# A decoder trunk step: another order of the first loads, the first squares later, and the second run of state steps one tile sooner

## The chip, the cores and the metric

The kernel runs on one core of a Trainium2 chip. The metric is the device time of one execution in microseconds. Two kernels are compared by the medians of their runs. One execution of each is taken with the hardware profiler; its trace gives the rows that are quoted. In them PE is TensorE's matmuls, PEld its weight loads, DVE VectorE, ACT ScalarE, POOL GpSimd, SP SyncE; a "q" behind an engine's name (SPq) is its sequencer issuing a DMA.

## The reference

One inference step of a trunk with a single layer: 512 new positions of one prompt and one new position of each of 8 samples, 520 columns in all, of 1024 channels, in fp32.

```python
h = h + 0.5 * swiglu(rms_norm(h, ffn1_norm), ffn1_w_gate, ffn1_w_up, ffn1_w_down)
h = h + hybrid_mixer(rms_norm(h, mix_norm), ...)      # pooling mixer and Mamba-2 SSD mixer side by side
h = h + 0.5 * swiglu(rms_norm(h, ffn2_norm), ffn2_w_gate, ffn2_w_up, ffn2_w_down)
y = rms_norm(h, final_norm)
# swiglu(x, wg, wu, wd) = (silu(x @ wg) * (x @ wu)) @ wd, with 2816 hidden channels
# outputs: y of prompt and samples, and the new pooling, convolution and SSM states of both
```

The new SSM state of a sample is state * decay + (dt * x) outer B, for 16 heads of 64 x 128.

## The kernel before, in words

**Layout.** `h` keeps the residual stream in SBUF, channels on the 128 partitions: 8 tiles of [128, 520], named by `d`. A tile of columns is halved (2 x 260). Tile d of the input x comes by one DMA from SP's queue (L500; the first one brings the vectors of parameters as well).

**An FFN.** There are 22 gate/up tiles `f` of 128 hidden channels each. The raw weights of one, `raw_f`, are two halves of [128, 1024] fp32, the gate's (u = 0) and the up's (u = 1); `raw` has two buffers, so a load waits until the tile two places before it has been used up. For most tiles the product is made in fp32r: every operand is split into a high part (a cast on ScalarE, L113) and a low part (a subtraction on VectorE, L114), `mm3` makes three matmuls of them (L124, L127, L128: high x high, high x low, low x high), and a scheme of seven products instead of eight combines column halves and weight halves (products 1 to 7 into the banks A and BE). For that the weights are summed first on VectorE (`sums`, L305 to L307, tiles `s`), and the sums are split too: `whi_fa`, `whi_fb` are casts of raw weights, `shi_fc`/`slo_fc` and `shi_fd`/`slo_fd` those of the sums. Copies of banks on ScalarE (`ac`, L344) let a bank be used again.

**The prologue.** Since normalised, split input isn't ready at once, FFN1's first two tiles, f = 0 and f = 1, are made in plain fp32 (`plain`, L254) from `xg`, which is x times the norm's weights without the root of the mean square; that factor is put on afterwards. One plain call is a matmul of 260 columns that shows as two records. The loop over j = 0..3 (L497 to L507) treats the pair of x tiles (j, j+4). For each j it does, as written: load both x tiles; load that part of raw_0 which this pair needs, u0 and u1, 128 KB each (L240; for j = 0 both from ScalarE's queue, else from SP's); scale (`scaled`, L192, ScalarE); square and sum the squares (`squares`, L161 and L164 on ScalarE, L165 on VectorE); the plain calls of f = 0, four of u0 and four of u1; and `prep_pair`, which forms the differences of the seven products and splits them into `xth`, `xtl` (L198 to L207, VectorE and ScalarE; the last pair's second half is kept for later, `late`). Then raw_1 is loaded (L236), the sum of squares goes through a matmul with ones (L170, tile `psr`) for each column half, ScalarE takes the root (L171), VectorE the reciprocal, and ScalarE copies the banks P of f = 0 into `tg` and `ac` (`keep`, L264; L267 for f = 1). The plain calls of f = 1 take the banks tagged A for u = 0 and the tag BE, which has two buffers, for u = 1: so these calls need the banks of f = 0 copied. The tile f = 2 follows by the seven products.

**The order.** The program is written in one order, and a scheduler decides each engine's own order from its idea of durations; `high_priority` moves a piece ahead, `queued(ins)` puts a piece behind the given instructions in an engine's order, `keep_in_program_order` pins one. On the chip every engine then runs its list strictly in order, and waits for what it needs.

**Down and the states.** `down` adds up the hidden tiles in chunks of 8, 8 and 6 (c = 0, 1, 2); in each it goes over the 8 output tiles d: load the weights, split them (`whi_d`, `wlo_d`), matmuls into the bank `dn`, then `td` and the addition to h on VectorE (L414, L418). In FFN2 the steps of `new_states` (L890 to L914) are put between these tiles, 16 in all, 8 in each of the first two chunks. `STATES[d]` says how many steps stand ahead of tile d. A step loads the broadcast row `br` and the state `hs` of the step after next from GpSimd's queue (L893, L895), makes four `so` on ScalarE (L909) and four `hs` on VectorE (L911), and writes `hs` out from GpSimd's queue (L913).

Of the kernel before, what the change touches and what calls it, by code (L numbers as in the profile page):

```python
# [11 lines left out]
AF = mybir.ActivationFunctionType  # L12
# [8 lines left out]
NT = SEQ + NS  # L21
HB = NT // 2
HALVES = (slice(0, HB), slice(HB, NT))
KD = D // P
# [9 lines left out]
CHUNKS = (8, 8, 6)  # L34
NG = 9
ON_ACT = 4
STATES = (0, 1, 1, 1, 2, 1, 1, 1)

CONV_PLAN = (
    "b0 b1 d0 b2 b3 x0 x1 v0 d1 x2 x3 d2 X0 p0 y0 c0 A0 p1 x4 m0 x5 B0 c1 p2 m1 A1 x6 c2 p3 A2 B1 x7 "  # L40
# [18 lines left out]
NVEC = _o  # L59
# [3 lines left out]
def tile_trunk_step(ctx: ExitStack, tc: tile.TileContext, ins: dict, outs: dict):  # L63
    nc = tc.nc

    def pool(name, side, **kw):
        return tc.alloc_tile_pool(name=name, bufs=1, side=side, reuse_waits="tile", **kw)
# [11 lines left out]
    vx = act.tile([P, NVEC + KD * NT], F32, tag="h", name="h")  # L79
# [3 lines left out]
    def v(name, i, n=P):  # L83
        return vec[:n, VEC[name] + i : VEC[name] + i + 1]
# [6 lines left out]
    def queued(*ins):  # L91
        stack = ExitStack()
        for i in ins:
            stack.enter_context(tc.issue_after(i))
        return stack
# [4 lines left out]
    half, ends = [], []  # L100
# [17 lines left out]
    def load_unit(src, n, name):  # L118
        raw = raw_tile(name)[:, :n]
        nc.sync.dma_start(out=raw, in_=src)  # L120
        return split(raw, n, name, wp, 3, ("whi", "wlo"))

    def mm3(ps, whi, wlo, xhi, xlo, start, stop, pin=False, **kw):
        first = nc.tensor.matmul(ps, whi, xhi, start=start, stop=False, **kw)  # L124
        if pin:
            tc.keep_in_program_order(first)
        nc.tensor.matmul(ps, whi, xlo, start=False, stop=False, **kw)  # L127
        nc.tensor.matmul(ps, wlo, xhi, start=False, stop=stop, **kw)  # L128

    def ws(w, k, m=P):  # L130
        return w[:, k * m : (k + 1) * m]
# [27 lines left out]
    def squares(nx, wx, d, name):  # L159
        if d == 0:  # L160
            nc.scalar.activation(out=nx[2], in_=h[:, d], func=AF.Square)  # L161
            return
        sq = wx.tile([P, 2, HB], F32, tag="tg", bufs=2, name=f"sq_{name}_{d}").rearrange("p b t -> p (b t)")
        nc.scalar.activation(out=sq, in_=h[:, d], func=AF.Square)  # L164
        nc.vector.tensor_tensor(out=nx[2], in0=nx[2], in1=sq, op=ALU.add)  # L165
# [17 lines left out]
    def new_xt(xp, name):  # L183
        return (xp.tile([P, KD // 2, 7, HB], F32R, tag="xth", name=f"xth_{name}"),
                xp.tile([P, KD // 2, 7, HB], F32R, tag="xtl", name=f"xtl_{name}"), *stat(name))

    def scaled(gp, nb, norm, j, name, halves=False):
        xg = gp.tile([P, 4, HB], F32, tag="g", bufs=nb, name=f"xg_{name}{j}")
        for d, out in ((j, xg[:, 0::3]), (j + KD // 2, xg[:, 1:3])):
            hd = h[:, d].rearrange("p (b t) -> p b t", b=2)  # L190
            for s in (slice(0, 1), slice(1, 2)) if halves else (slice(0, 2),):
                nc.scalar.activation(out=out[:, s], in_=hd[:, s], func=AF.Copy, scale=v(norm, d))  # L192
        return xg

    def prep_pair(nx, gp, nb, xg, j, name, late=None):
        xth, xtl, _, _ = nx
        xd = gp.tile([P, 4, HB], F32, tag="g", bufs=nb, name=f"xd_{name}{j}")
        nc.vector.tensor_tensor(out=xd[:, 0:2], in0=xg[:, 0::2], in1=xg[:, 3:4].to_broadcast([P, 2, HB]),  # L198
                                op=ALU.subtract)
        nc.vector.scalar_tensor_tensor(out=xd[:, 2], in0=xd[:, 1], scalar=-1.0, in1=xg[:, 0], op0=ALU.mult,  # L200
                                       op1=ALU.subtract)
        last = nc.vector.scalar_tensor_tensor(out=xd[:, 3], in0=xd[:, 2], scalar=-1.0, in1=xg[:, 1], op0=ALU.mult,
                                              op1=ALU.subtract)

        def parts(s, t):
            cast = nc.scalar.copy(xth[:, j, t], s)
            low = nc.vector.tensor_tensor(out=xtl[:, j, t], in0=s, in1=xth[:, j, t].bitcast(F32), op=ALU.subtract)  # L207
            return cast.ins, low.ins

        parts(xg[:, 0:3], slice(0, 3))  # L210
        if late is not None:
            late.append(lambda: parts(xd, slice(3, 7)))
            return None
        return last.ins, *parts(xd, slice(3, 7))

    class Ffn:
# [180 lines left out]
        def down(self, c, lo, hi, after):  # L397
            n = hi - lo
            banks, units = {}, {}

            def part(d, ks):
                if d not in units:
                    units[d] = load_unit(ins[f"w{self.i}d"][d, :, lo * P : hi * P], n * P, f"{self.i}d{d}_{c}")
                    banks[d] = ps[0].tile([P, 2, 512], F32, tag="BE", bufs=2, name=f"dn{self.i}_{d}_{c}")
                wh, wl = units[d]
                for b in range(2):
                    for k in ks:
                        g = self.g[lo + k]
                        mm3(banks[d][:, b, :HB], ws(wh, k), ws(wl, k), g[:, 0, b], g[:, 1, b], k == 0, k == n - 1)

            def done(d):
                t = self.wx.tile([P, 2, HB], F32, tag="tg", bufs=2, name=f"td{self.i}_{d}_{c}")
                hd = h[:, d].rearrange("p (b t) -> p b t", b=2)
                nc.vector.scalar_tensor_tensor(out=t, in0=banks[d][:, :, :HB], scalar=-0.5,  # L414
                                               in1=self.nx[3].rearrange("p (b t) -> p b t", b=2), op0=ALU.mult,
                                               op1=ALU.mult)
                if after is None:
                    nc.vector.tensor_tensor(out=hd, in0=t, in1=hd, op=ALU.add)  # L418
                    return
                for b, hs in enumerate(HALVES):  # L420
                    nc.vector.tensor_tensor(out=h[:, d, hs], in0=t[:, b], in1=h[:, d, hs], op=ALU.add)
                    after(d, b, hs)

            first = 0
            if after is not None:
                part(0, range(n - 1))
                part(1, range(n - 1))
                part(0, range(n - 1, n))
                done(0)
                part(1, range(n - 1, n))  # L430
                done(1)
                first = 2
            for d in range(first, KD):
                for _ in range(STATES[d] if self.states is not None else 0):
                    next(self.states)
                part(d, range(n))
                done(d)
# [51 lines left out]
    wx1, g1 = pool("wx1", "right"), pool("g1", "right")  # L489
    ffn_psum("ppf1")  # L490
    nx1 = new_xt(xt1, "f1")
    ffn1 = Ffn(nx1, 1, wx1, g1, 2)
    xg1, late = [], []
    warm = bank("warm")
    for _ in range(8):
        nc.tensor.matmul(warm[:, :P], ones, ones, start=True, stop=True)
    for j in range(KD // 2):  # L497
        for d in (j, j + KD // 2):
            q = slice(NVEC + d * NT if d else 0, NVEC + (d + 1) * NT)
            nc.sync.dma_start(out=vx[:, q], in_=ins["x"][:, q])  # L500
        ffn1.plain_load(0, j, queue=nc.sync if j else nc.scalar)
        xg1.append(scaled(g1, NG, "ffn1_norm", j, "f1", not j))
        with tc.high_priority() if j else nullcontext():
            for d in (j, j + KD // 2):
                squares(nx1, wx1, d, "f1")
        ffn1.plain(0, xg1[j], j)
        prep_pair(nx1, g1, NG, xg1[j], j, "f1", late if j == KD // 2 - 1 else None)  # L507
    ffn1.plain_load(1)
    with tc.high_priority():
        root, recip = ffn1.scales()  # L510
# [38 lines left out]
    def fin(d, b, hs):  # L549
        nx = f2["ffn"].nx  # L550
        if b:
            with tc.high_priority():
                squares(nx, f2["wx"], d, "f2")
        j = d - KD // 2
        if j >= 0 and b:
            f2[j] = scaled(f2["xg"], 4, "ffn2_norm", j, "f2")
# [37 lines left out]
    todo, late = [], []  # L594
# [589 lines left out]
```

## Time and profile before

| | |
|---|---|
| median of 3 runs | 989.91 us (987.9 to 990.07) |
| the profiled execution | 989.39 us |
| its span in the trace | 987.5 us |
| PE busy | 971.4 us, 98% of the span |
| DVE, ACT, POOL busy | 81%, 56%, 9% |
| HBM traffic | 116 GB/s over the span |

The span runs from the first recorded instruction to the last; 1.89 us lie around it. The rows of a timeline are: start, duration, engine, line, operation, output <- inputs, shapes, the number of instructions put together in the row, and in brackets the idle time of the engine before it and what ended that. A row of the waits view has the waiting engine, tile and line, what it waited for, the sum in us, the number of times, and the longest. A row of the chain has start, duration and what the chain ran through. A row of the DMA view has the transfer, the queue, how many, the size of each, and the median time from issue to landing. A row of the windows view has the window, its length, the busy time of PE, PEld, DVE, ACT and POOL with the number of instructions, TensorE's granted clock, the busy share of the DMA engines, and GB/s.

### The profile page before, as it was taken

The numbers are of one execution on the slowest core, as the hardware profiler recorded it, in microseconds if no ns is written. First come the engines' busy times: TensorE is split into PE (matmuls) and PEld (weight loads), VectorE is DVE, ScalarE is ACT, GpSimd is POOL, SyncE is SP. The second block draws the span as 40 slices with busy tenths as digits, with TensorE's granted clock in tenths as the row PEclk, the third lists the DMA queues.
The fourth block names the chain that finished last, engine by engine and source line by source line (L and its number), as shares of the span: only waits on it lengthen the run. The fifth ranks groups of instructions, "written<-read, shape, count | busy, mean of one in ns | idle before, by whom it ended". The sixth has DMA issues, their size and how long they took to land.

```text
span 987.5 us, 19451 instructions
## 1 busy us (share of the span) xinstructions
PE 971.4 (98%) x7868; PEld 952.7 (96%) x7868; DVE 797.8 (81%) x1288; ACT 555.7 (56%) x1019; POOL 89.6 (9%) x160
## 2 busy tenths in 40 slices
PE   8999999999999999999999999999999999999996
PEld 7999999999999999999899999999999999999995
DVE  6999656997569688789978997999967899668876
ACT  7766414664136455685668574666643566534653
POOL 0000000000000000156512000200012000120000
PEclk9999999999999999999999999999999999999998
DMA  5423322323222232262335232523346423453222
GB/s 181 167 90 103 112 87 85 129 86 129 86 87 81 91 126 88 82 199 106 124 113 188 73 134 86 151 103 129 110 122 197 150 94 121 123 180 121 93 65 88
DMA packets 42459, 115.53 MB, mean 117 GB/s; under 512 B 6456, under 2 KB 13560, under 8 KB 42368
## 3 DMA queue, kind: packets, MB, share of 16 engines
q1 hardware_dynamic: 38320, 103.52, 30.6%
q0 software_dynamic: 3504, 10.49, 4.0%
q8 instruction: 62, 1.02, 0.4%
q10 hardware_dynamic: 544, 0.26, 0.1%
q14 instruction: 29, 0.24, 0.1%
HBM read 106.91 MB, written 7.34 MB: 116 GB/s over the span
## 4 chain that ended last, share of the span: by engine, by line
PE 91%; DVE 4%; DMA 2%; ACT 1%; issue 1%; POOL 1%; DVEq 0%; ACTq 0%; SPq 0%
PE A L128 8%; PE A L124 8%; PE A L127 8%; PE dn L128 7%; PE dn L124 7%; PE dn L127 7%; PE BE L128 6%; PE BE L127 6%; PE BE L124 6%; PE P L254 4%; PE wo L124 2%; PE wo L128 2%; PE wo L127 2%; PE inz L124 2%; PE inz L128 2%; PE inz L127 2%
## 5 line engine op out<-in xcount | busy, mean ns | idle before, releaser
L127 PE MATMUL dn<-g,whi_1d 128*128 128x260 f32 x352 | 99.4, 282 | 0.0
L124 PE MATMUL dn<-g,whi_1d 128*128 128x260 f32 x352 | 99.2, 282 | 0.2 <-DVE td L414 0.2
L128 PE MATMUL dn<-g,wlo_1d 128*128 128x260 f32 x352 | 99.3, 282 | 0.0
L414 DVE SCALAR_TENSOR_TENSOR td<-dn,r_f 128x520 f32<-128x520 f32 x40 | 27.9, 699 | 72.7 <-PE dn L128 72.7
L128 PE MATMUL dn<-g,wlo_2d 128*128 128x260 f32 x256 | 72.6, 283 | 0.9 <-DVE wlo_2d L114 0.9
L127 PE MATMUL dn<-g,whi_2d 128*128 128x260 f32 x256 | 72.3, 282 | 0.0
L124 PE MATMUL dn<-g,whi_2d 128*128 128x260 f32 x256 | 72.3, 282 | 0.0
L124 PEld LDWEIGHTS dn<-g,whi_1d 128*128 128x128 f32 x352 | 66.1, 188 | 0.4 <-DVE td L414 0.4
L128 PEld LDWEIGHTS dn<-g,wlo_1d 128*128 128x128 f32 x352 | 66.3, 188 | 0.0
L127 PEld LDWEIGHTS dn<-g,whi_1d 128*128 128x128 f32 x352 | 66.2, 188 | 0.0
L344 ACT COPY ac<-A 128x260 f32<-128x260 f32 x123 | 45.6, 373 | 31.9 <-PE A L128 30.5
L113 ACT CAST whi_1d<-raw_1d 128x1024 fp32r<-128x1024 f32 (+1 forms) x24 | 23.4, 980 | 66.7 <-PE dn L127 54.1
L305 DVE TENSOR_TENSOR s<-raw 128x1024 f32<-128x1024 f32 x40 | 48.8, 1220 | 5.8 <-DMA raw<-in_w2gu 5.7
L128 PEld LDWEIGHTS dn<-g,wlo_2d 128*128 128x128 f32 x256 | 48.2, 188 | 1.1 <-DVE wlo_2d L114 1.1
L124 PEld LDWEIGHTS dn<-g,whi_2d 128*128 128x128 f32 x256 | 48.3, 189 | 0.0
L127 PEld LDWEIGHTS dn<-g,whi_2d 128*128 128x128 f32 x256 | 48.2, 188 | 0.0
L254 PE MATMUL P<-xg_f,raw 128*128 128x260 f32 x192 | 43.9, 383 | 1.7 <-DMA raw<-in_w1gu 1.7
L254 PEld LDWEIGHTS P<-xg_f,raw 128*128 128x128 f32 x192 | 35.9, 191 | 7.1 <-DMA raw<-in_w1gu 2.1
L124 PE MATMUL wo<-catg,whi_wo 128*128 128x260 f32 x128 | 37.2, 291 | 0.0
L124 PE MATMUL inz<-xh_mx,whi_inz 128*128 128x260 f32 x128 | 36.8, 287 | 0.0
L124 PE MATMUL inx<-xh_mx,whi_inx 128*128 128x260 f32 x128 | 36.4, 285 | 0.0
L128 PE MATMUL wo<-catg,wlo_wo 128*128 128x260 f32 x128 | 36.2, 283 | 0.0
(1350 smaller groups left out, 3949.5 us busy)
## 6 DMA issues: line engine op xcount, KB each, us to landing
raw<-in_w2gu SPq DMA_DIRECT2D x44, 512.0 KB, 4.5
raw<-in_w1gu SPq DMA_DIRECT2D x42, 512.0 KB, 4.4
raw_1d<-in_w1d SPq DMA_DIRECT2D x16, 512.0 KB, 4.4
raw_2d<-in_w2d SPq DMA_DIRECT2D x16, 512.0 KB, 4.4
raw_wo<-in_w_out SPq DMA_DIRECT2D x12, 512.0 KB, 4.7
ab<-scr_acs SPq DMA_DIRECT2D x8, 512.0 KB, 3.9
h<-in_state_ssm SPq DMA_DIRECT2D x16, 256.0 KB, 4.2
raw_inz<-in_w_in SPq DMA_DIRECT2D x8, 512.0 KB, 3.9
```

The lines of the kernel that those rows point to most:

```text
L113: cast = nc.scalar.copy(h, src)
L124: first = nc.tensor.matmul(ps, whi, xhi, start=start, stop=False, **kw)
L127: nc.tensor.matmul(ps, whi, xlo, start=False, stop=False, **kw)
L128: nc.tensor.matmul(ps, wlo, xhi, start=False, stop=stop, **kw)
L254: nc.tensor.matmul(self.banks[f, u][b][:, :HB], ws(self.raw[f][:, u], j + 4 * q), xg[:, slot[q]], start=j == q == 0, stop=j == 3 and q == ...
L305: nc.vector.tensor_tensor(out=s1, in0=diag, in1=up0, op=ALU.add)
L344: nc.scalar.copy(keep, out[:, :HB])
L414: nc.vector.scalar_tensor_tensor(out=t, in0=banks[d][:, :, :HB], scalar=-0.5, in1=self.nx[3].rearrange("p (b t) -> p b t", b=2), op0=ALU.mult,
```

## The change

- The loads of the prologue go out in another order: for each j the x tile j, then u0, then u1 of the weights, then the x tile j + 4. For j = 0 only u0 is left on ScalarE's queue; u1 goes out on SP's.
- `scaled` stands under `high_priority` for every pair, and it notes its first scaling instruction in `ends`.
- Squares and `prep_pair` of pair 0 are written in the turn j = 1; the squares of pair 0 are queued behind the first scaling of pair 1 (`ends`), without priority. The other pairs' are as before.
- `STATES` has one list for each of the two chunks. The first is as before, (0, 1, 1, 1, 2, 1, 1, 1); the second is (1, 1, 1, 1, 2, 1, 1, 0), so a step that stood ahead of one tile stands ahead of the tile before it.

No matmul is added or taken away, and no byte is loaded more or less.

```diff
-STATES = (0, 1, 1, 1, 2, 1, 1, 1)
+STATES = ((0, 1, 1, 1, 2, 1, 1, 1), (1, 1, 1, 1, 2, 1, 1, 0))
...
             for s in (slice(0, 1), slice(1, 2)) if halves else (slice(0, 2),):
-                nc.scalar.activation(out=out[:, s], in_=hd[:, s], func=AF.Copy, scale=v(norm, d))
+                done = nc.scalar.activation(out=out[:, s], in_=hd[:, s], func=AF.Copy, scale=v(norm, d))
+            if d == j:
+                ends[:] = [done.ins]
...
-                for _ in range(STATES[d] if self.states is not None else 0):
+                for _ in range(STATES[c][d] if self.states is not None else 0):
                     next(self.states)
...
+    def x_load(d):
+        q = slice(NVEC + d * NT if d else 0, NVEC + (d + 1) * NT)
+        nc.sync.dma_start(out=vx[:, q], in_=ins["x"][:, q])
+
     for j in range(KD // 2):
-        for d in (j, j + KD // 2):
-            q = slice(NVEC + d * NT if d else 0, NVEC + (d + 1) * NT)
-            nc.sync.dma_start(out=vx[:, q], in_=ins["x"][:, q])
-        ffn1.plain_load(0, j, queue=nc.sync if j else nc.scalar)
-        xg1.append(scaled(g1, NG, "ffn1_norm", j, "f1", not j))
-        with tc.high_priority() if j else nullcontext():
-            for d in (j, j + KD // 2):
-                squares(nx1, wx1, d, "f1")
+        x_load(j)
+        ffn1.plain_load(0, j, (0,), nc.sync if j else nc.scalar)
+        ffn1.plain_load(0, j, (1,))
+        x_load(j + KD // 2)
+        with tc.high_priority():
+            xg1.append(scaled(g1, NG, "ffn1_norm", j, "f1", not j))
+        for k in ((), (0, 1), (2,), (3,))[j]:
+            with tc.high_priority() if k else queued(*ends):
+                for d in (k, k + KD // 2):
+                    squares(nx1, wx1, d, "f1")
         ffn1.plain(0, xg1[j], j)
-        prep_pair(nx1, g1, NG, xg1[j], j, "f1", late if j == KD // 2 - 1 else None)
+        for k in ((), (0, 1), (2,), (3,))[j]:
+            prep_pair(nx1, g1, NG, xg1[k], k, "f1", late if k == KD // 2 - 1 else None)
```

## The prediction, made before the changed kernel ran

> **What bounds the kernel now.** I read first the page's busy times and shares of the chain that ended last, then TensorE's waits, then TensorE's timeline through the prologue. The profiled execution took 989.39 us, 987.5 of it the span, 1.89 around it; the median of the runs is 989.91 (987.9 to 990.07).
>
> ```profile
> span 987.5 us, 19451 instructions
> PE 971.4 (98%) x7868; PEld 952.7 (96%) x7868; DVE 797.8 (81%) x1288; ACT 555.7 (56%) x1019; POOL 89.6 (9%) x160
> PE 91%; DVE 4%; DMA 2%; ACT 1%; issue 1%; POOL 1%; DVEq 0%; ACTq 0%; SPq 0%
> ```
>
> ```profile
> PE P L254 <- DMA raw<-in_w1gu: 1.7, 1, 1.7
> PE dn L128 <- DVE wlo_2d L114: 0.9, 1, 0.9
> PE BE L124 <- ACT ac L344: 0.6, 1, 0.6
> ```
>
> ```profile
> 4.63 1.08 PE L254 MATMUL P<-xg_f,raw 128*128 128x260 f32 x4
> 7.37 17.80 PE L254 MATMUL P<-xg_f,raw 128*128 128x260 f32 x80 [1.65 <-DMA raw<-in_w1gu]
> 25.01 1.04 PE L170 MATMUL psr_f<-acc_f,ones 128*128 128x260 f32 x4
> 25.89 9.81 PE L254 MATMUL P<-xg_f,raw 128*128 128x260 f32 x44
> ```
>
> TensorE is busy 98% of the span and is 91% of the chain, so nothing that only speeds another engine counts; only TensorE's waits do. The change keeps every matmul and goes for two of those waits: 1.65 us at 5.7 for the second half of the first weights (u1), and 0.9 us in FFN2's `down` behind the state steps. One plain fp32 call is two records: 80 records from 7.37 to 25.01 are 40 calls of 0.441 us. That is the yardstick below. TensorE's calls have one fixed order, so a wait shifts all that follows it.
>
> **Part 1, the front.** In after u1 is the second DMA on SP's queue instead of the second on ScalarE's, and TensorE alternates u0 and u1 calls on the first tile.
>
> ```profile
> 1.39 5.94 DMA raw<-in_w1gu
> raw<-in_w1gu ACTq DMA_DIRECT2D x2, 128.0 KB, 3.5
> h<-in_x SPq DMA_DIRECT2D x1, 320.0 KB, 3.0
> 0.74 2.02 SPq L500 DMA_DIRECT2D h<-in_x  x4
> 3.79 0.91 ACT L192 ACTIVATE xg_f<-h 128x260 f32<-128x260 f32 x2 [0.46 <-DMA h<-in_x]
> 7.14 0.64 ACT L164 ACTIVATE sq_f<-h 128x520 f32<-128x520 f32 x1 [0.58 <-DMA h<-in_x]
> 10.30 1.07 SPq L236 DMA_DIRECT2D raw<-in_w1gu  x2
> raw<-in_w1gu SPq DMA_DIRECT2D x2, 512.0 KB, 5.5
> 12.41 1.35 ACT L192 ACTIVATE xg_f<-h 128x520 f32<-128x520 f32 x2
> 3.00:15.50 12.50, 10.85 (x50) 9.33 (x50) 9.28 (x15) 11.47 (x21) 0.00 (x0) 1.00 0.98 319
> ```
>
> SP issues one DMA each 0.5 us (4 in 2.02), so u1 goes out at about 1.25 and lands, with 3.0 to 3.5, at 4.3 to 4.8: the wait of 1.65 goes, and TensorE runs from 4.63. Pair 0 and pair 1 are 16 calls, so call 17 (pair 2) is due at 4.63 + 16 x 0.441 = 11.69; before it came at 7.37 + 14 x 0.441 = 13.54.
>
> What is late next is ScalarE. Pair 2's first scaled tile (the row at 12.41) stands behind the same 14 ScalarE instructions in both kernels: scaling, squares and casts of pairs 0 and 1, from 3.79. Between 3.79 and 12.41 ScalarE idled only 0.58, so it can start no earlier than 11.83, and it is a chain through x tiles that land at 0.98 DMA share. I take 12.6 (12.41, plus 0.2 since u1's 128 KB now goes ahead of x tiles on SP's queue), ready 0.7 later at 13.3. So call 17 waits 1.6 us for ScalarE where call 5 waited 1.65 for the DMA. Behind it, the seven calls on f=1 that now stand among pair 2's need raw_1's first half, SP's load at 10.30 landing 5.5 later by the median of its two halves, the first somewhat sooner. The bytes ahead of it are the same, and 319 GB/s at 0.98 share leaves no room: call 21 comes at about 15.2; before, it came at 7.37 + 18 x 0.441 = 15.31. **Front: -0.1 us**; bounds -1.8 (nothing late: the whole wait is won) and +0.6 (tiles 0.6 later). I stay near no gain because both rows, 12.41 and 10.30 + 5.5, are the same work in both kernels.
>
> The moved squares and `prep_pair` of pair 0 cost VectorE and ScalarE nothing more (same instructions, inside the same 14), and the new wait on pair 1's first scaling is in ScalarE's own order.
>
> [...]
>
> **Part 2, the middle.** The scheduler's order changes around the sum of squares (psr), and this is where I find the cost.
>
> ```profile
> 24.33 0.33 SPq L286 DMA_DIRECT2D raw<-in_w1gu  x1
> 35.72 3.71 DMA raw<-in_w1gu
> 25.65 0.92 ACT L171 ACTIVATE r_f<-psr_f,eps 128x260 f32<-128x260 f32 x2 [4.37 <-PE psr_f L170]
> 26.46 0.58 ACT L264 COPY tg<-P 128x520 f32<-128x520 f32 x1
> 28.38 1.06 ACT L113 CAST whi_2a<-raw 128x1024 fp32r<-128x1024 f32 x1
> ```
>
> Before: ScalarE does both roots, then copies tg from bank P of f=0 (done 27.04). The first P call of f=1's second half needs that bank; it stands 6 calls after psr, at 25.89 + 6 x 0.441 = 28.5. The copy had 1.5 us to spare.
>
> After: psr stands behind 45 calls, not 42, so 3 calls lie between it and that P call, not 6; and on ScalarE the cast whi_2a stands **between the two roots**, ahead of the tg copy. whi_2a waits for raw_2, whose load waits until the last f=0 call frees its buffer: call 41 (before call 40). Working: call 21 at 15.2, 45 calls done at 15.2 + 25 x 0.441 = 26.2; call 41 ends at 15.2 + 21 x 0.441 = 24.46; SP issues raw_2 0.2 later, at 24.7, and its first half takes 3.7 (row 35.72, the same size of load): 28.4. whi_2a 28.4 to 29.4, second root to 29.75, tg copy to 30.35, so the P call starts at 30.4. It is due at 26.2 + 0.88 (psr, 25.01 to 25.89) + 3 x 0.441 = 28.4. **+2.0**, and 0.1 for the restart.
>
> ```profile
> raw<-in_w1gu SPq DMA_DIRECT2D x4, 512.0 KB, 4.6
> 36.10 0.43 SPq L287 DMA_DIRECT2D raw<-in_w1gu  x1
> 40.42 0.36 ACT L344 COPY ac<-BE 128x260 f32<-128x260 f32 x1
> 39.45 1.22 DVE L114 TENSOR_TENSOR slo_2d<-s,shi_2d 128x1024 fp32r<-128x1024 f32 x1
> 40.78 1.22 DVE L305 TENSOR_TENSOR s<-raw 128x1024 f32<-128x1024 f32 x1
> 40.83 0.39 PE L124 MATMUL BE<-xth_f,shi_2d 128*128 128x260 f32 x1 [0.56 <-ACT ac L344]
> 41.18 0.28 PE L128 MATMUL A<-xth_f,slo_2d 128*128 128x260 f32 x1
> ```
>
> A second wait follows on VectorE. Before, slo_2d (39.45) stands ahead of s (40.78), the first sum over raw_3; after, s stands ahead. The loads at 35.72 and 36.10 follow the plain calls' end, so all of this shifts by 2.0: the loads go out at 37.7 and 38.1, the ac copy that TensorE waited 0.56 for comes 2.0 later (that wait stays as it is), and slo_2d is due at 41.18 + 2.0 = 43.2. But s waits for raw_3's second half, 38.1 + 4.6 = 42.7, runs to 43.9, and slo_2d ends at 45.1: **+1.95**, and 0.1 for the restart. In before slo_2d was done in time because it waited for no load.
>
> The other reorderings of the built program here (BE_3's products ahead of A_2's last, a swap between A_5 and A_4) keep TensorE fed by tiles that are ready, so they cost nothing; if one isn't ready its price is a cast, 1.0.
>
> **Part 3, the states.** FFN2's second `down` has its steps one tile sooner.
>
> ```profile
> 875.12 0.33 SPq L286 DMA_DIRECT2D raw<-in_w2gu  x1
> 881.09 1.28 ACT L909 ACTIVATE so<-br,sxdt 128x128 f32<-128x128 f32 x4 [3.94 <-DMA br<-scr_bc]
> 884.99 1.28 ACT L909 ACTIVATE so<-br,sxdt 128x128 f32<-128x128 f32 x4 [2.36 <-DMA br<-scr_bc]
> 886.18 1.03 ACT L113 CAST whi_2d<-raw_2d 128x1024 fp32r<-128x1024 f32 x1
> 883.53 1.23 DVE L305 TENSOR_TENSOR s<-raw 128x1024 f32<-128x1024 f32 x1 [3.73 <-DMA raw<-in_w2gu]
> 887.47 1.13 DVE L911 SCALAR_TENSOR_TENSOR hs<-hs,sdec,so 128x128 f32<-128x128 f32 x4
> 888.52 1.22 DVE L114 TENSOR_TENSOR wlo_2d<-raw_2d,whi_2d 128x1024 fp32r<-128x1024 f32 x1
> 888.00:890.00 2.00, 1.08 (x9) 0.88 (x8) 2.00 (x5) 0.62 (x1) 0.55 (x1) 1.00 0.06 25
> ```
>
> TensorE has 9 matmuls in 888 to 890 where 0.12 us each would make 17: a loss of 1.0 to 1.2, for the last tile's wlo (888.52). Its cast whi ended at 887.2, held by the so step at 884.99, which waits for its br row. With the step one tile sooner that cast ends near 883.4. But wlo's own place on VectorE is behind s (883.53), which waits 3.73 for the next gate/up load, issued at 875.12 and landed at 883.4. From there VectorE runs without a gap to 888.52: three sums, td, h, four hs, wlo. None of it waits for whi. In after the same chain stands ahead of wlo, and the load has the same bytes around it. **0**; bounds -1.2 (the stall goes) and +0.7 (the step's copy moved into 881.09's place pushes TensorE's other waits).
>
> **Sum:** -0.1 + 2.1 + 2.05 + 0 = +4.05; 989.39 + 4.05 = 993.4 us. All that follows 45 us is TensorE-bound (the 98% above), with no later wait for a load that could take the shift back, so it carries to the end.
>
> **Rivals.**
> 1. Not slower by what can be measured: the head start at the front is kept. x tiles land sooner than I take, ScalarE has pair 2 ready by 11.7 and raw_1's first half is there by 13.4. For: u1 no longer goes out late, and 11.83 is all but enough. Against: 0.98 DMA share. Front -1.8 in place of -0.1; the middle keeps its waits, since raw_2's load and psr move with the calls. 993.4 - 1.75 = 991.65, inside 0.2% of 989.91.
> 2. The states pay: the gate/up load lands earlier, by about 882, since fewer POOL transfers lie beside it, and wlo is in time. For: a br load and a step are gone from those microseconds. Against: DMA share is low there (0.06 at 888), yet the load took 8 us. -1.2: 992.2.
> 3. u1 lands no sooner than before: TensorE still starts its u1 calls at 7.4, and now after fewer calls, since u0 and u1 alternate. Calls run then from 7.37 with one done, call 17 at 7.37 + 15 x 0.441 = 13.99 in place of 13.54: front +0.45 in place of -0.1: 994.0. [...] Against: ScalarE's queue had u1 second, SP's has it second of 16 behind one tile.
>
> **How the numbers follow.** Forecast 0.52, rival 1 0.13, rival 2 0.18, rival 3 0.14, something not seen 0.03. 0.2% is 1.98 us, about what a measurement of this kernel tells from no change. The range goes from 991.0 (rival 1 with 0.65 of the states) to 994.8 (forecast with the states' +0.7 and half of the front's +0.6 and the restarts). Faster by over 0.2% needs rival 1 and 2 together and half the middle gone: 0.05. Within 0.2% (up to 991.9): rival 1 and part of rival 2, 0.15. Slower: 0.80.
>
> **What would show it.** In the profile after: TensorE's 1.7 on the DMA gone, and a wait of about 1.5 on ScalarE's xg near 12 in its place; whi_2a between two roots with idle time on raw ahead of it, and TensorE waiting about 2 for tg near 28.4 to 30.4; a wait of about 1.9 for slo_2d near 43 to 45; the 0.9 for wlo_2d still there. It is wrong if tg or slo_2d doesn't show, or if call 17 starts by 12.

## The result, and the profile after

The changed kernel took 994.22 us (median of 6 runs, 992.66 to 995.57) against 989.0 for the kernel before (6 runs, 987.9 to 990.07): a ratio of 1.0053, with a 95% interval of 1.0039 to 1.0067. That is slower by 5.2; the forecast was 993.4. The profiled execution took 994.35, its span 992.6, which is 5.1 more.

The page first: of the 5.1, TensorE's busy time holds 1.5 (972.9 against 971.4) and its idle time 3.6. A part of the waiting shows as busy time: the first row of TensorE's timeline below gives 5.91 to 24 records, where 12 calls of 0.441 are 5.29. No matmul was added, so I read the 5.1 as waits.

```profile
span 992.6 us, 19445 instructions
PE 972.9 (98%) x7868; PEld 952.3 (96%) x7868; DVE 798.0 (80%) x1288; ACT 556.2 (56%) x1019; POOL 89.9 (9%) x160
```

TensorE's waits in the kernel after:

```profile
PE P L256 <- ACT tg L266: 1.6, 1, 1.6
PE A L128 <- DVE slo_2d L114: 1.6, 1, 1.6
PE P L256 <- ACT xg_f L192: 1.5, 2, 1.4
PE dn L128 <- DVE wlo_2d L114: 0.9, 1, 0.9
PE P L256 <- DMA raw<-in_w1gu: 0.4, 1, 0.4
```

The wait of 1.7 for u1 is gone. In its place stand xg, tg, slo_2d and a wait for raw_1; the 0.9 in `down` is still there. Where they lie, in TensorE's timeline of the kernel after:

```profile
4.60 5.91 PE L256 MATMUL P<-xg_f,raw 128*128 128x260 f32 x24
10.70 2.02 PE L256 MATMUL P<-xg_f,raw 128*128 128x260 f32 x8 [0.19 <-ACT xg_f L192]
14.07 2.02 PE L256 MATMUL P<-xg_f,raw 128*128 128x260 f32 x8 [1.35 <-ACT xg_f L192]
16.50 11.22 PE L256 MATMUL P<-xg_f,raw 128*128 128x260 f32 x50 [0.41 <-DMA raw<-in_w1gu]
27.56 1.04 PE L170 MATMUL psr_f<-acc_f,ones 128*128 128x260 f32 x4
28.44 1.48 PE L256 MATMUL P<-xg_f,raw 128*128 128x260 f32 x6
31.57 6.62 PE L256 MATMUL P<-xg_f,raw 128*128 128x260 f32 x29 [1.65 <-ACT tg L266]
```

TensorE runs from 4.60 without the old gap, but pair 2 (call 17) starts at 14.07, later than the 13.54 worked out for before, and call 21 at 16.50 instead of 15.31. ScalarE's timeline of the kernel after shows both ends of this:

```profile
3.83 0.92 ACT L192 ACTIVATE xg_f<-h 128x260 f32<-128x260 f32 x2 [1.14 <-DMA h<-in_x]
6.17 1.53 ACT L192 ACTIVATE xg_f<-h 128x260 f32<-128x260 f32 x3 [1.43 <-DMA h<-in_x]
7.61 0.62 ACT L161 ACTIVATE acc_f<-h 128x520 f32<-128x520 f32 x1
...
13.29 1.34 ACT L192 ACTIVATE xg_f<-h 128x520 f32<-128x520 f32 x2
...
28.20 0.48 ACT L171 ACTIVATE r_f<-psr_f,eps 128x260 f32<-128x260 f32 x1 [5.54 <-PE psr_f L170]
29.61 1.04 ACT L113 CAST whi_2a<-raw 128x1024 fp32r<-128x1024 f32 x1 [0.93 <-DMA raw<-in_w1gu]
30.56 0.47 ACT L171 ACTIVATE r_f<-psr_f,eps 128x260 f32<-128x260 f32 x1
30.93 0.58 ACT L266 COPY tg<-P 128x520 f32<-128x520 f32 x1
```

At 4.7 ScalarE stands still for 1.43 until x tile 4 lands. The first square (L161) used to run just there (4.61 before); now it is queued behind pair 1's scaling and comes at 7.61. Further down whi_2a sits between the two roots with 0.93 of idle time on raw_2 ahead of it, and the tg copy ends at 31.5.

To see where time is lost and where not, I take the same weight load on SP's queue in both kernels. A load is issued as TensorE frees its buffer, so it marks TensorE's progress; the table gives the issue time less that of before, from each kernel's profiled execution. In the first column 0.4 of the figures of after, e1 and e4 is not lost time: the load follows call 41 there, not call 40. The columns from 35.72 on have no such difference.

| load issued before at | 24.33 | 35.72 | 55.90 | 605.70 | 686.14 | 862.09 | 930.70 |
|---|---|---|---|---|---|---|---|
| after | +1.7 | +3.2 | +5.2 | +5.0 | +5.0 | +5.1 | +5.0 |
| e1 prologue alone | +1.2 | +2.7 | +6.2 | +5.8 | +5.8 | +5.8 | +6.1 |
| e2 states alone | -1.0 | -1.0 | -1.1 | -1.5 | -1.5 | -1.5 | -2.7 |
| e3 loads alone | -0.2 | -0.2 | -0.3 | -0.7 | -0.7 | -0.7 | -0.7 |
| e4 two orders pinned | +1.6 | +1.2 | +2.6 | +1.8 | +2.8 | +2.8 | +2.4 |
| e5 squares moved alone | -0.1 | +4.6 | +8.2 | +7.7 | +7.7 | +7.6 | +7.6 |
| e6 e4, psr sooner | +0.7 | +0.7 | +0.8 | +0.2 | +1.3 | +1.3 | +0.1 |
| e12 all but the move | +0.1 | +0.1 | +0.2 | -0.6 | -0.6 | -0.6 | -1.2 |

For after, everything is lost by 56 us, and nothing comes back. Each row is one execution. e2 has the prologue of before unchanged, and its load at 24.33 still goes out 1.0 sooner, as its u1 was waited for 0.8 and not 1.7; in e7, with the same prologue, it goes out 0.1 sooner. So a shift of 1 at the front can be chance.

### The profile page after: what moved, and what is told of

It is laid out like the page before. It is cut to its first block, busy times and chain, and to the rows that moved or that the text cites. A ratio compares the mean times of both kernels' runs of the same rounds, so it can differ in the third digit from the quotient of the medians.

```text
span 992.6 us, 19445 instructions
## 1 busy us (share of the span) xinstructions
PE 972.9 (98%) x7868; PEld 952.3 (96%) x7868; DVE 798.0 (80%) x1288; ACT 556.2 (56%) x1019; POOL 89.9 (9%) x160
## 4 chain that ended last, share of the span: by engine, by line
PE 87%; DMA 4%; DVE 4%; issue 1%; ACT 1%; SPq 1%; POOL 1%; DVEq 0%; POOLq 0%; ACTq 0%
PE A L128 8%; PE A L124 8%; PE A L127 8%; PE dn L128 6%; PE dn L124 6%; PE dn L127 6%; PE BE L128 6%; PE BE L127 6%; PE BE L124 6%; PE P L256 3%; PE wo L124 2%; PE wo L128 2%; PE wo L127 2%; PE inz L124 2%; PE inz L128 2%; PE inz L127 2%
```

## The experiments

The before of each run is that of its own chip and session (988.5 to 988.9).

**e1: the prologue's edits without the states** (against the changed kernel).

```diff
-STATES = ((0, 1, 1, 1, 2, 1, 1, 1), (1, 1, 1, 1, 2, 1, 1, 0))
+STATES = (0, 1, 1, 1, 2, 1, 1, 1)
...
-                for _ in range(STATES[c][d] if self.states is not None else 0):
+                for _ in range(STATES[d] if self.states is not None else 0):
```

> The changed kernel with the old STATES in both runs: the prologue's edits alone. My theory: the state steps do nothing, so this is as slow as the changed kernel, 5.1 us above the kernel before (994.1), with the same three waits of TensorE (for xg and raw_1 near 12 to 16, for tg 1.6, for slo_2d 1.6). Rival: the state steps won their 1.2 and the prologue costs more than the waits show; then this is at 995.3. Second rival: the steps cost part of the 5; then this is 1 us or more under the changed kernel, 993 or less.

Measured: 995.39 (6 runs), ratio 1.0063 (1.0049 to 1.0076). The three waits are there as expected (xg 1.8, tg 1.6, slo_2d 1.4), and the prologue carries the whole loss. The median is that of the first rival, but the profile doesn't show its cause: the wait for the last wlo is 0.8 here and 0.9 in after. The profiled execution is 1.0 longer than that of after, and the table shows that it lost this between 35.72 and 55.90, where its waits are not longer. The windows view of e1 tells why; its columns are the window, its length, the busy times, and last TensorE's granted clock, DMA share, GB/s:

```profile
43.00:46.00 3.00, 0.84 (x4) 0.56 (x4) 2.67 (x3) 1.26 (x3) 0.00 (x0) 0.97 0.84 317
46.00:49.00 3.00, 3.00 (x15) 3.00 (x15) 2.71 (x4) 0.38 (x1) 0.00 (x0) 0.50 0.00 0
49.00:52.00 3.00, 3.00 (x26) 3.00 (x25) 1.77 (x2) 1.77 (x2) 0.00 (x0) 0.96 0.74 228
```

Behind the waits for ac and slo_2d TensorE was busy but got half its clock: 15 matmuls in 3 us, 26 in the next 3; by the table that lost 1.4. In the kernel after the same stretch looks like this:

```profile
43.00:46.00 3.00, 1.03 (x6) 0.60 (x4) 2.17 (x3) 1.71 (x3) 0.00 (x0) 1.00 0.94 309
46.00:49.00 3.00, 2.65 (x22) 2.65 (x23) 2.96 (x5) 0.45 (x2) 0.00 (x0) 1.00 0.11 44
```

Its clock stayed at 1.00. So the medians of e1 and after can't be set against each other to price the states.

**e2: the states alone, and e7: two tiles sooner** (against the kernel before).

```diff
-STATES = (0, 1, 1, 1, 2, 1, 1, 1)
+STATES = ((0, 1, 1, 1, 2, 1, 1, 1), (1, 1, 1, 1, 2, 1, 1, 0))   # e2
+STATES = ((0, 1, 1, 1, 2, 1, 1, 1), (1, 1, 1, 1, 2, 2, 0, 0))   # e7
...
```

> The kernel before with only the second STATES list. My theory: 0, 989.0 within 0.6, and TensorE's wait of 0.9 for the last wlo stays, since VectorE's chain behind the gate/up load (three sums, td, h, four hs) stands ahead of it all the same. Rival: the wait goes, -1.2, 987.8.

> The kernel before with the second list (1, 1, 1, 1, 2, 2, 0, 0): the last steps two tiles sooner, so that no hs stands on VectorE between h and the last wlo (1.13 shorter chain behind the gate/up load). My theory: the wait of 0.9 for the last wlo is set by VectorE's chain behind that load; here it goes even where the load takes 7.9 us: -0.9, 988.0. Rival: the wait moves to another tile (so step or br row), or the load comes later by as much: 989 and the wait is in the profile.

Measured: e2 988.46 (12 runs), ratio 0.9994 (0.9985 to 1.0004); e7 989.1 (11 runs), 1.0001 (0.9992 to 1.001). In both profiles the wait for the last wlo is gone, which in e2 goes against my theory. e7 doesn't test its own: its gate/up load took 6.4 by the median of its two halves, so the wait may have gone for the reason that it went in e2. Which reason that is, the profiles of all runs narrow down. In before, the br load that the new list moves goes out beside the gate/up load (issued at 875.12):

```profile
876.76 0.54 POOL L895 DMA_DIRECT2D hs<-in_state_ssm  x1 [2.41 <-DMA out_nss<-hs]
877.84 0.54 POOL L893 DMA_DIRECT2D br<-scr_bc  x1
raw<-in_w2gu SPq DMA_DIRECT2D x2, 512.0 KB, 7.5
```

In e9 (below), which has the new list, no br load goes out there, and in e2 neither:

```profile
874.46 0.33 SPq L286 DMA_DIRECT2D raw<-in_w2gu  x1
876.13 0.54 POOL L899 DMA_DIRECT2D hs<-in_state_ssm  x1 [2.50 <-DMA out_nss<-hs]
raw<-in_w2gu SPq DMA_DIRECT2D x2, 512.0 KB, 7.3
```

```profile
873.64 0.33 SPq L286 DMA_DIRECT2D raw<-in_w2gu  x1
874.32 0.54 POOL L895 DMA_DIRECT2D hs<-in_state_ssm  x1 [1.53 <-DMA out_nss<-hs]
raw<-in_w2gu SPq DMA_DIRECT2D x2, 512.0 KB, 6.1
```

The missing br alone hardly matters: in before and e9 hs goes out 1.6 and 1.7 behind the load, with and without br, and the load takes 7.5 and 7.3. What goes with the load's time is how soon hs goes out behind it:

| | old list: before, e1, e3, e5 | after | e9 | e4 | e12 | e7 | e10 | e2, e6, e8, e11 |
|---|---|---|---|---|---|---|---|---|
| hs issued behind the load | 1.6 to 2.0 | 2.2 | 1.7 | 1.3 | 1.2 | 1.2 | 1.1 | 0.7 |
| the load's median time | 7.4 to 7.5 | 7.5 | 7.3 | 7.1 | 6.9 | 6.4 | 5.6 | 5.8 to 6.1 |
| TensorE's wait for wlo | 0.8 to 0.9 | 0.9 | 0.7 | 0.5 | 0.3 | 0 | 0 | 0 |

hs waits in its turn for an earlier hs to be written out (out_nss), so its place differs from run to run. That an early hs makes the load short is the likeliest reading; no run isolates it. With the old list the wait is 0.8 to 0.9, four times of four; over the nine profiles with the second list of the change its mean is 0.27, a win of about 0.6. But five of the nine (e4, e6, e8, e10, e11) also have other orders in FFN2 (e4's pin, below); over the other four (after, e2, e9, e12) the mean is 0.5, a win of about 0.4. After's profile happened to be the one in which the states won nothing. The times can't tell such a win from 0, and e7's list isn't told apart from the others by them either.

**e3: the new loads alone, and e9: loads and states.** Squares, `prep_pair` and priorities as before; the diff is against the kernel before.

```diff
...
-        for d in (j, j + KD // 2):
-            q = slice(NVEC + d * NT if d else 0, NVEC + (d + 1) * NT)
-            nc.sync.dma_start(out=vx[:, q], in_=ins["x"][:, q])
-        ffn1.plain_load(0, j, queue=nc.sync if j else nc.scalar)
+        x_load(j)
+        ffn1.plain_load(0, j, (0,), nc.sync if j else nc.scalar)
+        ffn1.plain_load(0, j, (1,))
+        x_load(j + KD // 2)
```

> The kernel before with only the new order of the prologue's loads (x j, u0, u1, x j+4; u1 of the first pair on SP's queue); squares, prep_pair and STATES as before. The scheduler then leaves both roots together, six plain calls behind psr and slo_2d ahead of s. My theory: the u1 wait goes and ScalarE's pair 2 takes its place (1.2 to 1.6 for xg near 12); no wait for tg and none for slo_2d; 989.0 to 989.8. Rival: the order of the loads itself is what costs (raw_1 landing about 1 us later, 16.45 against 15.39): then about 990.2 or more. Second rival: without the moved squares the head start is kept, -1.5: 987.5.

> The new order of the loads and the new STATES, with squares, prep_pair and priorities as in the kernel before. My theory: e3's gain (0.5) stands, and of the states' wait of 0.9 a part goes, as the gate/up load lands sooner in most executions with the new list (6.3 to 7.5 us in four profiles, 7.9 in one, against 7.9 with the old list): 987.6 to 988.4. Rival: the states bring nothing in the mean: 988.4 to 989.

Measured: e3 988.42 (12 runs), 0.9989 (0.9979 to 0.9998); e9 988.02 (11 runs), 0.9998 (0.9989 to 1.0007). The loads aren't to blame. TensorE in e3:

```profile
4.32 2.02 PE L254 MATMUL P<-xg_f,raw 128*128 128x260 f32 x8
6.54 2.02 PE L254 MATMUL P<-xg_f,raw 128*128 128x260 f32 x8 [0.20 <-ACT xg_f L192]
9.35 3.77 PE L254 MATMUL P<-xg_f,raw 128*128 128x260 f32 x16 [0.80 <-ACT xg_f L192]
13.34 11.66 PE L254 MATMUL P<-xg_f,raw 128*128 128x260 f32 x52 [0.22 <-ACT xg_f L192]
24.84 1.04 PE L170 MATMUL psr_f<-acc_f,ones 128*128 128x260 f32 x4
```

The 1.65 for u1 has become 1.2 of waits for ScalarE, pair 2 starts at 13.34, and psr stands behind 42 calls: no wait for tg, none for slo_2d.

**e5: the other half of the prologue.** Against the changed kernel: old loads and old STATES; `scaled` under priority, squares and `prep_pair` of pair 0 moved, as in the change.

```diff
...
-        x_load(j)
-        ffn1.plain_load(0, j, (0,), nc.sync if j else nc.scalar)
-        ffn1.plain_load(0, j, (1,))
-        x_load(j + KD // 2)
+        for d in (j, j + KD // 2):
+            q = slice(NVEC + d * NT if d else 0, NVEC + (d + 1) * NT)
+            nc.sync.dma_start(out=vx[:, q], in_=ins["x"][:, q])
+        ffn1.plain_load(0, j, queue=nc.sync if j else nc.scalar)
```

> The other half of the prologue's edit: loads in their old order (u1 on ScalarE's queue), but scaled under priority and the squares and prep_pair of pair 0 moved; STATES as before. The scheduler then puts psr behind 46 plain calls with two to the P call that needs tg, whi_2a ahead of both roots, and s ahead of slo_2d. My theory: the cost lies here. The u1 wait stays; raw_2 goes out at 24.1 as before and lands at 28.0, whi_2a ends at 29.0, then the table load (1.3), two roots and the tg copy to 31.8, for a P call due at 28.5: 3.3; slo_2d late by 1 to 2: 993.2 to 994.3. Rival: the loads are to blame and this is as the kernel before, 988.5 to 990.

Measured: 996.95 (4 runs), 1.0082 (1.0068 to 1.0096). The cost lies here, and it is larger than I worked out. ScalarE in e5 has the expected order, within 0.3 of the expected times:

```profile
27.81 1.04 ACT L113 CAST whi_2a<-raw 128x1024 fp32r<-128x1024 f32 x1 [7.66 <-DMA raw<-in_w1gu]
28.87 1.28 ACT L171 ACT_TABLE_LOAD   x1
30.16 0.84 ACT L171 ACTIVATE r_f<-psr_f,eps 128x260 f32<-128x260 f32 x2
30.90 0.59 ACT L266 COPY tg<-P 128x520 f32<-128x520 f32 x1
```

slo_2d, expected 1 to 2 late, was waited for only 0.3; waits of 1.2 for ac and 0.6 for shi_2d stand in its place. What I hadn't counted is the clock. TensorE waited 3.01 for tg, and then:

```profile
27.00:31.00 4.00, 1.54 (x8) 0.98 (x6) 0.33 (x1) 3.16 (x5) 0.00 (x0) 1.00 0.30 123
31.00:34.00 3.00, 2.46 (x6) 1.98 (x7) 3.00 (x2) 3.00 (x7) 0.00 (x0) 0.52 0.00 0
...
45.00:48.00 3.00, 1.25 (x6) 0.83 (x7) 2.65 (x3) 1.86 (x4) 0.00 (x0) 1.00 0.94 326
48.00:52.00 4.00, 4.00 (x22) 4.00 (x22) 2.74 (x4) 0.50 (x2) 0.00 (x0) 0.57 0.16 36
```

Two dips, of 1.5 and 1.7 (in the first, 16 calls took 8.74, where the same 16 took 7.28 in after; in the second 4 us at 0.57). Without these 3.2 the 8.2 of the table would be 5.0, the expected size.

**e4: the two orders pinned, and e6: psr sooner as well** (against the changed kernel).

```diff
-        ffn1.behind[2] = ((ffn1.plain_out(0),),) * 2 + (False,)
+        scaled_tg = ffn1.plain_out(0)
+        ffn1.behind[2] = (copied, scaled_tg), (scaled_tg,), False
...
-                self.behind[3] = tuple(ends), (), False
+                self.behind[3] = tuple(ends), tuple(ends), False
```

```diff
+            summed[:] = [nc.tensor.matmul(ps, ones, sq, start=k == 0, stop=k == len(acc) - 1).ins]   # e6, in rstd
...
+            with queued(*(summed if u or j > 1 else ())):   # e6
+                ffn1.plain(1, xg1[j], j, (u,))
```

> The changed kernel with two orders pinned: whi_2a on ScalarE behind the copies of f = 0's banks, and the sums of raw_3 on VectorE behind slo_2d. My theory: the waits for tg (1.65) and slo_2d (1.6) and their restarts go, 3.5 to 3.9 off: 990.3 to 990.7; the front's 1.2 is left. Rival: the waits are only where a bound of the loads shows, and others take their place (whi_2a or wlo_2a late for A_2, raw_3 late for s): then 992 or more.

> As e4_both_fix, and psr's two matmuls pinned behind 40 plain calls instead of 45 (f = 1's calls of u = 0 for pairs 2 and 3 queued behind them). e4 left 2.8, with new waits for shi_2d (0.7) and slo_2d (0.8) where VectorE's chain from the reciprocals on (28.7, 3.4 us for the two) runs late. My theory: that chain hangs on psr's place in TensorE's order; 5 calls are 2.2 us, so both waits go: 990.0 to 990.6, the front's 0.9 to 1.2 left. Rival: the chain hangs on raw_2's load, or the sum of squares isn't ready so soon (TensorE then waits for acc): 991.5 or more.

Measured: e4 991.77 (8 runs), 1.0028 (1.0018 to 1.0037); e6 990.57 (11 runs), 1.0023 (1.0014 to 1.0032). e4's waits:

```profile
PE P L256 <- ACT xg_f L192: 2.3, 3, 1.4
PE A L128 <- DVE slo_2d L114: 0.8, 1, 0.8
PE A L124 <- ACT shi_2d L113: 0.7, 1, 0.7
```

The time is above the 990.3 to 990.7 of my theory. The wait for tg is gone, but the rival was half right: slo_2d is only halved and shi_2d appears, since VectorE's chain from the reciprocals on hangs on psr, which stands three calls later. With psr pinned ahead (e6) both go and +0.7 of the front is left at 35.72. The table shows a second thing: e4 and e6 lose 1.0 between 605.70 and 686.14. The pin stands in code that FFN2 runs too, and there it put slo_2d ahead of s where the other order was the better one. So e6 met its numbers partly for a wrong reason: 1.0 of its 2.0 is a cost of the experiment itself.

**e8, e10, e11: tries at a better version.** e8: squares of pair 0 at once, other squares and `prep_pair` behind the scaling of pair 2 or 3, f = 1's calls behind f = 0's, pins as in e6. e10: e9 with e6's pins and the squares' additions on GpSimd. e11: e8 with the same.

```diff
-        nc.vector.tensor_tensor(out=nx[2], in0=nx[2], in1=sq, op=ALU.add)
+        (nc.gpsimd if name == "f1" else nc.vector).tensor_tensor(out=nx[2], in0=nx[2], in1=sq, op=ALU.add)
```

> A version from what the runs showed: the new loads and STATES; squares of pair 0 at once (in ScalarE's idle time while x tile 4 lands), all other squares and prep_pair behind the scaling of pair 2 or 3; f = 1's calls behind the last call of f = 0, psr behind 40 calls; whi_2a behind the copies, the sums of raw_3 behind slo_2d. My theory: the front's waits (xg 1.2 in e3) go down to 0.3, the middle's stay at those of the kernel before: 986.5 to 987.5. Rival: TensorE's head start is lost again to VectorE's chain (prep_pair now late, acc or slo_2c late): 988 to 990.

> As e9, with the additions of FFN1's squares on GpSimd (which is idle there) instead of VectorE, psr behind 40 plain calls, and whi_2a and the sums of raw_3 pinned as in e4. My theory: VectorE's work through the prologue (adds, prep_pair, reciprocals) is what takes a head start back; with 7 adds of 0.7 off it and psr sooner, slo_2c's 0.4 and ac's 0.4 go: 986.5 to 987.6. Rival: GpSimd's adds are slow and psr waits for acc: 989 or more.

> As e8, with the additions of FFN1's squares on GpSimd. e8 lost its front gain to a wait of 1.57 of psr for acc on VectorE. My theory: that wait goes, and TensorE keeps 1 us more of its head start: 986.5 to 988. Rival: GpSimd's adds take as long, or the copies to xtl are the last thing on VectorE and f = 2 waits for them: 989.5 or more.

Measured: e8 990.55 (11 runs), 1.0027 (1.0018 to 1.0035); e10 990.41 (11 runs), 1.0022 (1.0013 to 1.0031); e11 992.65 (5 runs), 1.0042 (1.003 to 1.0055). All three missed their forecasts, and all carry FFN2's 1.0. In e8 TensorE was 0.5 ahead of before by the end of call 40 (23.6 against 24.1, at 0.441 a call), and psr, which stands there, then waited for VectorE's additions:

```profile
PE psr_f L170 <- DVE acc_f L165: 1.6, 1, 1.6
```

Both tries with GpSimd failed: one addition took 1.28 or more there against 0.7 on VectorE, and e11's wait of psr grew to 2.9.

**e12: the whole change but the moved squares and `prep_pair`** (against the changed kernel).

```diff
...
-        for k in ((), (0, 1), (2,), (3,))[j]:
-            with tc.high_priority() if k else queued(*ends):
-                for d in (k, k + KD // 2):
-                    squares(nx1, wx1, d, "f1")
+        with tc.high_priority() if j else nullcontext():
+            for d in (j, j + KD // 2):
+                squares(nx1, wx1, d, "f1")
...
-        for k in ((), (0, 1), (2,), (3,))[j]:
-            prep_pair(nx1, g1, NG, xg1[k], k, "f1", late if k == KD // 2 - 1 else None)
+        prep_pair(nx1, g1, NG, xg1[j], j, "f1", late if j == KD // 2 - 1 else None)
```

> The whole change but one part: squares and prep_pair of pair 0 stay where the kernel before has them (loads, priority of scaled and STATES are the new ones). Written out, psr stands behind 42 calls again, both roots together ahead of whi_2a, slo_2d ahead of s. My theory: the moved squares are the whole cost, through the orders that the scheduler makes of them and through ScalarE's idle time while x tile 4 lands: 987.6 to 988.6. Rival: the priority of scaled carries part of it: 990 or more.

Measured: 988.34 (12 runs), 1.0001 (0.9992 to 1.0009). With squares and `prep_pair` of pair 0 back in their place the 5.2 are gone: the move is the whole cost. Which of the two moved pieces makes the scheduler's new orders, no run shows. Three kernels have the new loads without the move (e3, e9, e12): 0.9989, 0.9998, 1.0001. Only the first lies clear of 1, so a version that beats the kernel before isn't shown.

## Why the prediction was right, and where it wasn't

- **Front, -0.1 forecast: +1.2 measured** (call 21 at 16.50, forecast 15.2). This step failed, and outside its bound of +0.6. The prediction said that the moved squares "cost VectorE and ScalarE nothing more (same instructions, inside the same 14)", and took 0.58 as ScalarE's idle time. But x tile 4 is the third DMA on SP's queue now and lands at 6.1; behind pair 1's scaling the squares can't fill the 1.43 until then, and pair 2's scaling starts at 13.29 where 12.6 was taken. Of the 1.2, 0.5 is pair 2 (14.07 against 13.54) and the rest raw_1, which landed at 16.5, 6.8 after its issue, where 15.2 was taken; e1 shows no wait for raw_1 and comes to call 21 at 16.07 (+0.8), so this part varies, as does before's own front (1.0 sooner in e2).
- **tg, +2.1 forecast: +2.0 measured** (3.16 less 1.19, the table's shift at 35.72 less the front's). Right in mechanism and size: wait 1.65, whi_2a between the roots, P call at 31.57.
- **slo_2d, +2.05 forecast: +2.1 measured** (5.23 less 3.16). Right. VectorE in the kernel after:

```profile
43.93 1.23 DVE L307 TENSOR_TENSOR s<-raw 128x1024 f32<-128x1024 f32 x1 [0.83 <-DMA raw<-in_w1gu]
45.08 1.22 DVE L114 TENSOR_TENSOR slo_2d<-s,shi_2d 128x1024 fp32r<-128x1024 f32 x1
```

s waits for raw_3 and slo_2d behind it, as worked out. e4 adds what the prediction didn't see: pinning the order alone doesn't heal it, because psr is late too. The prediction gives no source for the 0.1 of a restart; in the rows the first matmul behind a wait took 0.39 (before at 40.83, after at 44.24 and 46.35) and the next ones 0.28 or 0.29.
- **States, 0 forecast: 0 in after's profile, about -0.4 to -0.6 on average over all profiles.** The step "the load has the same bytes around it" was wrong: with the new list a br load is missing there, and where hs goes out sooner the gate/up load is up to 1.9 shorter (5.6 in e10 against 7.5). Rival 2's wait that goes is seen in five of the nine profiles with the second list, but of the four without other orders in FFN2 only in e2. That the term came out at 0 in after was luck.
- **Carried to the end: right.** +5.2 at 55.90, +5.0 at 930.70.
- Rival 1 (head start kept) fell at 14.07, rival 3 (u1 no sooner) at 5.05: there TensorE loaded its first weights of u1, after 0.26 of idle time for them. (The 3.5 that the prediction took for u1's load was the median of u0 and u1, of which u1 alone took 5.94; u1 now took 3.8.) u1 went out at 1.19 on SP's queue, ahead of x tile 4 (1.92); before, at 1.39 on ScalarE's. Whether the other queue or the other place in the order of issue brought it sooner, no run shows.

The forecast added 4.05 and the profiled execution 5.0; the front's error (+1.3) is more than the difference, and the others are 0.1 to 0.2 each, so no large errors cancelled. That after's profile had no dip of the clock, which cost e1 1.4 and e5 3.2, the prediction had not weighed; there too it was lucky.

## What to carry to other kernels

Where a scheduler writes the engines' orders, read the new orders ahead of pricing the edit: 4 of the 5 us here were lost by no instruction that the change moved, but by a cast that slipped between two roots and a sum that slipped ahead of a subtraction. The other 1 went because squares that had filled a hole in ScalarE's time were moved and nothing else could fill it: filler work is worth moving only if something else fits its hole. And a pin that mends one place belongs under a condition for that place, as e4's cost in FFN2 shows.

## What the runs showed of the hardware

- **A cluster of waits can cost more than its length.** Behind a stretch in which TensorE was busy 0.84 of 3 us (e1), its granted clock was 0.50 over the next 3 us, in which it was fully busy. Behind 1.54 of 4 us (e5) it was 0.52 over 3 us (busy 2.46), and behind 1.25 of 3 (e5 again) 0.57 over 4 (fully busy). By the estimates above, 1.4 to 1.7 were lost each time on top of the waits. In e1 TensorE wasn't wholly idle in the stretch: it ran 4 matmuls there. After's stretch (1.03 of 3) brought no dip, though its two waits (0.71 and 1.60) were longer than e1's (0.71 and 1.44), and neither did e11's (0.33 of 3, behind which the clock stayed at 1.00). Why like stretches ended differently, no run here shows. Whether after's slower runs (up to 995.57) had such a dip, no trace here shows.
- **The time of one weight load, 5.6 to 7.5, went with when another transfer was issued.** With hs issued 0.7 to 1.1 us behind it, 1 MB of weights took 5.6 to 6.1 by the median of its halves; with hs 1.6 to 2.2 behind it, 7.3 to 7.5. This goes together over the fourteen profiles and isn't isolated.
- **VectorE was slower beside GpSimd's additions.** While these ran in e11, a subtraction of 520 columns took 1.78 on VectorE; the same subtraction took 0.70 while GpSimd stood still. GpSimd and VectorE in e11:

```profile
19.42 7.72 POOL L165 TENSOR_TENSOR acc_f<-acc_f,sq_f 128x520 f32<-128x520 f32 x4 [3.70 <-ACT sq_f L164]
```

```profile
12.34 0.70 DVE L198 TENSOR_TENSOR xd_f<-xg_f 128x520 f32<-128x520 f32 x1 [0.92 <-ACT xg_f L192]
21.98 1.78 DVE L198 TENSOR_TENSOR xd_f<-xg_f 128x520 f32<-128x520 f32 x1
```
